# Moving four modulation blocks of the second layer from TensorE in the recurrence to VectorE sums in the gating stage

## The chip, the cores and the metric

The kernel runs on one core of one Trainium2 chip. The metric is the device time of one execution in microseconds. The engines are TensorE (PE, the matmuls), VectorE (DVE), ScalarE (ACT), GpSimd (POOL) and SyncE (SP), which here only issues DMAs. Each has its own instruction queue and works through it in order.

## The reference

Two layers over 1024 latent tokens and 256 context tokens of width 1024 (W below is 512). Each layer scales and shifts its input by a modulation of the conditioning, mixes, and closes with a gated residual and a layer norm. The change touches the modulation of the second layer (l = 1) and two branches of the first layer's mixer.

```python
def modulation(cond, w, b):
    m = jax.nn.silu(cond) @ w + b
    shift, scale, gate = jnp.split(m[:, None, :], 3, axis=-1)
    return shift, scale, gate
...
def spatial_gating(u, v, ln_g, ln_b, w_s, b_s):
    bsz, n, _ = v.shape
    vh = layer_norm(v, ln_g, ln_b).reshape(bsz, n // SGU_CHUNK, SGU_CHUNK, SGU_GROUPS, SGU_GROUP_DIM)
    s = jnp.einsum('gpq,bnqgc->bnpgc', w_s, vh) + b_s.T[:, :, None]
    return u * s.reshape(bsz, n, BRANCH_WIDTH)
...
    def branches(pp, h_rec):
        y_a = h_rec.astype(pp.dtype) * jax.nn.silu(pp[..., W:2 * W])
        u = jax.nn.gelu(pp[..., 2 * W:3 * W])
        v = jax.nn.gelu(pp[..., 3 * W:4 * W])
        y_b = spatial_gating(u, v, sgu_ln_g, sgu_ln_b, sgu_w, sgu_b) * jax.nn.silu(pp[..., 4 * W:5 * W])
        return jnp.concatenate([y_a, y_b], axis=-1) @ w_out
...
def reference(...):
    for l in range(DEPTH):
        shift, scale, gate = modulation(c, w_mod[l], b_mod[l])
        shift_c, scale_c, gate_c = modulation(c_ctx[None], w_mod[l], b_mod[l])
        h = x * (1.0 + scale) + shift
        hc = ctx * (1.0 + scale_c) + shift_c
        ...
        x = layer_norm(DEEPNORM_ALPHA * x + gate * y, ln_g[l], ln_b[l])
```

h_rec in branches is the sum of two linear recurrences (RG-LRU), one in each direction. Its coefficients come from four gates per group of 128 channels, two for each direction.

## The kernel before

**Precision and weights.** Every projection is made in three passes: an operand is split into a rounded high part and the low rest, and hi·hi, hi·lo and lo·hi are summed in PSUM. wload (L143) fetches a weight by an SP DMA into wraw (2 buffers) and splits it in two halves: the high part whi by ACT, the low part wlo by POOL (4 buffers of each, so two weights' halves). One projection (proj3c_g, L167) takes 8 k steps for each of three column chunks of 256, 512 and 512 tokens.

**PSUM.** Two three-bank slots (pj3, tag "pj") are taken in turn by whatever asks next: projections px, pg, pu, pz, the gates pgate of the recurrence, and most value tiles pv. Two single banks (psb) serve the small products.

**The recurrence stage** runs px0 and pg0 (which overlap the loading of the input), px1, rec0, pg1, px2, rec1, pg2, px3, rec2, pg3, pu0, rec3, in PE's written order (PE is under a manual schedule; the other engines are ordered by the scheduler, SP by hand in two stretches). lru_x projects and convolves one group of channels, lru_g makes its silu gate, lru_rec makes four pgate tiles of nine matmuls. For each, ACT takes a tanh out of PSUM (gt), then for each direction a tanh tt and an exponential, DVE the rest; lru_scan takes square roots on ACT and scans on DVE. pu0 is the first group's u of the gating branch, made in a three-bank slot and emptied by three gelus into ut0.

**The modulation blocks.** A layer's modulation has six blocks of 512 columns: 0 and 1 shift, 2 and 3 scale, 4 and 5 gate. The eight blocks that this stage makes are listed in `blocks`. mod_load fetches one block's eight 256 KB tiles wm. mod_do makes it on PE with eight 32-row matmuls (modp, L221) of the silu vector csil, which leave four partial sums in four groups of 32 partitions; DVE copies them to mb. At the next mod_do, mod_c closes it: for blocks 0 to 3 by four transposes (modcp, L228) and a DVE reduction, for gate blocks by one small matmul (gatep, L495). mod_step is called at steps 9 and 17 of every projection of the stage, at the start of each recurrence and after each of its directions, and every third call does mod_do.

**The gating stage** runs pz0, pu1, ten value tiles pv0 to pv9 (sgu_v), pz1, pu2, pz2, pu3, pz3. A value tile goes through a gelu on ACT (vf), mean and variance on DVE, the power -1/2 on POOL, and a scaling on DVE. sgu_s multiplies it by the 128 x 128 spatial weights (sps) between later tiles' matmuls, the last two tiles between the matmuls of pz1. Each pz ends in a tanh on ACT and two products on DVE.

**The output projection** of the first layer (out0_a, out0_b, L683 to L685) follows in six single-bank tiles pout, which are laid over the PSUM that the pj slots leave. Its eight weights w_out 0 to 7 are split by POOL for 0 to 3 and by DVE for 4 to 7 (wol, at L141).

Of the kernel before, what the change touches and what calls it, by code (L numbers as in the profile page):

```python
# [10 lines left out]
F32 = mybir.dt.float32  # L11
# [31 lines left out]
def tile_hybrid_trunk(es: ExitStack, tc: tile.TileContext, A, out, scr=None):  # L43
# [99 lines left out]
    def wload(src, nk=8, le=None):  # L143
# [3 lines left out]
        for h in range(nk // 4):  # L147
            hi = wp.tile([128, 4, 128], F32R, name="whi", tag="whi", bufs=4)
            lo = wp.tile([128, 4, 128], F32R, name="wlo", tag="wlo", bufs=4)
            split(hi, lo, raw[:, 4 * h:4 * h + 4], le=le or G)  # L150
            res.append((hi, lo))
# [73 lines left out]
    def mod_cols(mb, out, bias, one):  # L225
        p = psb("modcp")
        for i in range(4):
            T.transpose(p[:, 128 * i:128 * i + 128], mb[:, 128 * i:128 * i + 128], ident)  # L228
        t = const.tile([128, 4, 2], F32, name="mct", tag="mct", bufs=2)
        V.tensor_reduce(t, p.rearrange("p (i g r) -> p i r g", g=4, r=32)[:, :, 0:2, :], axis=AX.X, op=ALU.add)  # L230
        for o, i0, i1, b, add in zip(out, (0, 2), (2, 4), bias, one):
            V.scalar_tensor_tensor(o, t[:, i0:i1, :], add, b[:, :, None].to_broadcast([128, i1 - i0, 2]),
                                   op0=ALU.add, op1=ALU.add)
# [132 lines left out]
    with pool("lrua") as lp, pool("lruc") as lc:  # L366
# [29 lines left out]
        def lru_g(f):  # L396
            if f:
                p = pj3("pg")
                PROJ(proj3c_g(p, wload(A["w_in0"][4 + f])))
# [87 lines left out]
        def mod_c(l, blk, mb):  # L487
            if blk < 4:
                s, j = divmod(blk, 2)
                k0 = 4 * j  # L490
                mod_cols(mb, [mod1[:, k0 + 2 * i:k0 + 2 * i + 2, s, :] for i in range(2)],
                         [P("bmod1")[:, 4 * blk + 2 * i:4 * blk + 2 * i + 2] for i in range(2)], (float(s),) * 2)
            else:
# [7 lines left out]
        blocks = [(0, 4), (0, 5)] + [(1, i) for i in range(6)]  # L501
# [3 lines left out]
        def mod_step():  # L505
            calls[0] += 1
            if calls[0] % 3 == 2:
                mod_do()
# [23 lines left out]
        p = pj3("pu")  # L532
        proj3(p, wload(A["w_in0"][8]))
        for c0, n in CHUNKS:
            S.activation(ut0[:, c0:c0 + n], p[:, 256 + c0:256 + c0 + n], AF.Gelu_apprx_tanh)
# [17 lines left out]
    V.scalar_tensor_tensor(zt0, zt0, 1.0, p[:, 256:1536], op0=ALU.add, op1=ALU.mult)  # L553
    gp_cm = pool("sgu")
# [5 lines left out]
    with pool("sguw") as vw:  # L560
# [4 lines left out]
        VF = [vw.tile([128, 512], F32, name=f"vf{i}") for i in range(6)]  # L565
# [7 lines left out]
        def sgu_v(t, between=None):  # L573
# [4 lines left out]
            vf = VF[t % 6]  # L578
# [697 lines left out]
```

## Time and profile before

| | |
|---|---|
| time, median of 3 runs (lowest to highest) | 1142.79 us (1142.55 to 1142.98) |
| the profiled execution, its time | 1142.13 us |
| its span, first to last instruction | 1140.3 us |
| granted TensorE clock, mean | 0.998 |
| PE busy | 1116.7 us, 98% |
| DVE busy | 720.9 us, 63% |
| ACT busy | 436.0 us, 38% |
| POOL busy | 284.6 us, 25% |

The profiled execution lies 0.66 us below the median, and 1.8 us of its time lie outside the span. Of the span, the recurrence stage with px1 onward and up to pz0 takes from 53.2 to 204.0 us, the gating stage from 204.0 to 365.8; the output projection and the second layer follow. In a timeline row the first two numbers are the start and the duration of a row's instructions from the first start to the last end; a row with xN holds N of them. Matmuls overlap: a 512-column one shows 0.39 us and the next starts 0.23 us after it.

### The profile page before, as it was taken

Reading aid. Unit: us, or ns where it says so; the run is one execution under the profiler, and the core shown is the slowest. Engines: PE = TensorE matmul, PEld = TensorE weight load, DVE = VectorE, ACT = ScalarE, POOL = GpSimd, SP = SyncE. Lnnn points to the kernel's source line nnn. Section 1 sums busy time; section 2 is a strip of 40 time slices with the busy share of each in tenths; the row PEclk is TensorE's granted clock in tenths of the full one; section 3 lists DMA queues with packets and bytes.
Section 4 is the critical chain, followed back from the end, with each engine's and each line's share of the span. In section 5 each row is a group of like instructions: output and inputs, shape, how many; then the busy total and the mean of one; then the engine's idle time right before and its main releaser. Section 6 shows DMA issues by size and latency. Waiting matters only on the chain.

```text
span 1140.3 us, 14964 instructions
## 1 busy us (share of the span) xinstructions
PE 1116.7 (98%) x5842; PEld 920.0 (81%) x5842; DVE 720.9 (63%) x1031; ACT 436.0 (38%) x687; POOL 284.6 (25%) x228
## 2 busy tenths in 40 slices
PE   6999999999999999999999999999999999999997
PEld 4777777888888888888788788888888888888886
DVE  6777986943412566537512876777676666738986
ACT  4463665620221243343212545444544444424210
POOL 0011112530240222258402322323421321220021
PEclk9999999999999999999999999999999999999999
DMA  9654542220241543336637243442531520127641
GB/s 368 258 178 157 185 154 105 94 97 1 86 142 54 180 152 116 120 130 208 230 93 190 91 112 78 111 118 65 143 96 40 144 91 20 48 73 240 203 148 74
DMA packets 78199, 148.08 MB, mean 130 GB/s; under 512 B 6305, under 2 KB 35873, under 8 KB 77233
## 3 DMA queue, kind: packets, MB, share of 16 engines
q1 hardware_dynamic: 71088, 128.25, 33.0%
q0 software_dynamic: 7040, 18.88, 7.3%
q8 instruction: 46, 0.75, 0.3%
q14 instruction: 25, 0.20, 0.1%
HBM read 112.49 MB, written 34.62 MB: 129 GB/s over the span
## 4 chain that ended last, share of the span: by engine, by line
PE 84%; DVE 5%; DMA 4%; issue 3%; ACT 3%; POOL 1%; SPq 0%; POOLq 0%; DVEq 0%; ACTq 0%
PE pout L683 5%; PE pout L685 5%; PE pout L684 5%; PE p L184 4%; PE p L185 4%; PE p L186 4%; PE psc L992 3%; PE pv L208 3%; PE pv L209 3%; PE pv L210 3%; PE psc L993 3%; PE atr L1015 3%; PE modp L221 2%; PE pz L172 2%; PE pz L174 2%
## 5 line engine op out<-in xcount | busy, mean ns | idle before, releaser
L141 POOL TENSOR_TENSOR wlo<-wraw,whi 128x512 fp32r<-128x512 f32 x86 | 134.3, 1565 | 427.8 <-ACT whi L138 415.6
L994 DVE TENSOR_REDUCE st<-psc 128x1 f32<-128x1280 f32 x64 | 95.1, 1486 | 39.5 <-PE psc L993 39.5
L683 PE MATMUL pout<-woh,yhi 128*128 128x512 f32 (+1 forms) x296 | 114.8, 388 | 0.3 <-DVE xres L1168 0.2
L685 PE MATMUL pout<-woh,ylo 128*128 128x512 f32 (+1 forms) x296 | 114.4, 386 | 0.0
L684 PE MATMUL pout<-wol,yhi 128*128 128x512 f32 (+1 forms) x296 | 114.1, 385 | 0.0
L996 ACT ACTIVATE e<-psc,st 128x1280 f32<-128x1280 f32 x64 | 85.2, 1331 | 71.7 <-DVE st L994 68.8
L184 PE MATMUL p<-hhl,whi 128*128 128x512 f32 x256 | 105.0, 410 | 0.0
L138 ACT ACTIVATE whi<-wraw 128x512 fp32r<-128x512 f32 x92 | 57.5, 628 | 122.8 <-PE p L185 27.2
L186 PE MATMUL p<-hhl,wlo 128*128 128x512 f32 x256 | 100.5, 393 | 0.0
L185 PE MATMUL p<-hll,whi 128*128 128x512 f32 x256 | 100.3, 392 | 0.0
L138 ACT ACTIVATE ah<-atr 128x512 fp32r<-128x512 f32 (+1 forms) x96 | 47.1, 525 | 64.6 <-PE atr L1015 64.2
L992 PE MATMUL psc<-k,qh 128*128 128x512 f32 (+1 forms) x192 | 67.1, 364 | 2.6 <-ACT e L996 2.5
L993 PE MATMUL psc<-k,ql 128*128 128x512 f32 (+1 forms) x192 | 68.7, 358 | 0.0
L683 PEld LDWEIGHTS pout<-woh,yhi 128*128 128x128 f32 x296 | 55.6, 188 | 12.4 <-issue 0.6
L685 PEld LDWEIGHTS pout<-woh,ylo 128*128 128x128 f32 x296 | 55.6, 188 | 11.6 <-DVE ylo L141 0.2
L684 PEld LDWEIGHTS pout<-wol,yhi 128*128 128x128 f32 x296 | 55.7, 188 | 11.3
L138 ACT ACTIVATE yhi<-yraw 128x512 fp32r<-128x512 f32 x36 | 22.5, 631 | 108.0 <-PE pout L684 72.3
L141 DVE TENSOR_TENSOR al<-atr,ah 128x512 fp32r<-128x512 f32 (+1 forms) x96 | 54.5, 594 | 6.3 <-ACT ah L138 6.2
L186 PEld LDWEIGHTS p<-hhl,wlo 128*128 128x128 f32 x256 | 48.0, 188 | 10.8
L185 PEld LDWEIGHTS p<-hll,whi 128*128 128x128 f32 x256 | 48.3, 189 | 8.2
L184 PEld LDWEIGHTS p<-hhl,whi 128*128 128x128 f32 x256 | 48.2, 188 | 8.0
L208 PE MATMUL pv<-wvh,hhl 128*128 128x512 f32 x128 | 52.0, 406 | 0.0
(325 smaller groups left out, 2815.8 us busy)
## 6 DMA issues: line engine op xcount, KB each, us to landing
wraw<-in_w_in_dram SPq DMA_DIRECT2D x42, 512.0 KB, 3.6
wm<-in_w_mod_dram SPq DMA_DIRECT2D x64, 256.0 KB, 4.7
wraw<-in_w_out_dram SPq DMA_DIRECT2D x16, 512.0 KB, 4.3
wm<-in_w_mod_dram SPq DMA_DIRECT2D x7, 1024.0 KB, 11.4
xt<-in_xcT_dram SPq DMA_DIRECT2D x8, 640.0 KB, 8.6
xres<-in_xc_dram SPq DMA_DIRECT2D x10, 512.0 KB, 4.0
wvr<-in_w_v_dram SPq DMA_DIRECT2D x8, 512.0 KB, 3.6
n_d<-xres SPq DMA_DIRECT2D x8, 512.0 KB, 2.6
```

The source lines that it names most:

```text
L138: S.activation(hi, src, AF.Copy)
L141: le.tensor_tensor(lo, src, f32(hi), op=ALU.subtract)
L184: T.matmul(o, hi[:, k % 4], hh[:, k], start=k == 0, stop=False)
L185: T.matmul(o, hi[:, k % 4], hl_[:, k], start=False, stop=False)
L186: T.matmul(o, lo[:, k % 4], hh[:, k], start=False, stop=k == KT - 1)
L208: T.matmul(p, hh[:, k], wh, start=k == 0, stop=False)
L683: T.matmul(o, hi[:, i], wh[:, c], start=first and i == 0, stop=False)
L684: T.matmul(o, hi[:, i], wl[:, c], start=False, stop=False)
L685: T.matmul(o, lo[:, i], wh[:, c], start=False, stop=not first and i == 3)
L992: T.matmul(o, qh[:, m, cu], KS[hd, m][:, c:c + n], start=True, stop=False)
L993: T.matmul(o, ql[:, m, cu], KS[hd, m][:, c:c + n], start=False, stop=True)
L994: V.tensor_reduce(st[:, m:m + 1], p[:, 256:1536], axis=AX.X, op=ALU.max, negate=True)
```

## The change

- Blocks 0 to 3 of the second layer leave the list `blocks`, and with them their modp, modcp, DVE copies and reductions. Four gate blocks stay; mod_step makes one at every fourth call instead of every third, so they move to other calls.
- mod_sums makes the four blocks in the gating stage. For each of the eight k it loads a 256 KB tile wmd (3 buffers) and DVE adds wmd times a column of csil to macc, once for each of the two conditionings: 64 DVE operations of 128 x 512. mod_rows then sums macc over the partitions on PE with eight one-column matmuls (modq) per block and one DVE addition. In PE's order the four groups stand after pv8, pu2, pz2 and pz3.
- DVE is put under a manual schedule for the value part; two sums are written between a tile's power and its scaling, and one after it.
- The gate branch's weights (pg1 to pg3) and u0's weight get whi and wlo buffers of their own in the pool lrua, two of each.
- u0 is projected chunk by chunk into single banks (psb) instead of a three-bank slot. Five vf tiles instead of six.
- One pj tile fewer is allocated, so from rec3 on each pj tile has the other slot, and the first pout lies on the banks of pz3 instead of pu3. The pool of xres and gl (residual and gate tiles of the output projection) now reuses memory that is free only after the gating stage; in SP's order their loads stand behind the store of pz3's result and ahead of w_out 6 and 7, where before they stood among the loads of pu2 and pz2.

```diff
-    def wload(src, nk=8, le=None):
+    def wload(src, nk=8, le=None, wq=None):
...
-            hi = wp.tile([128, 4, 128], F32R, name="whi", tag="whi", bufs=4)
-            lo = wp.tile([128, 4, 128], F32R, name="wlo", tag="wlo", bufs=4)
+            hi = (wq or wp).tile([128, 4, 128], F32R, name="whi", tag="whi", bufs=2 if wq else 4)
+            lo = (wq or wp).tile([128, 4, 128], F32R, name="wlo", tag="wlo", bufs=2 if wq else 4)
...
+    def mod_sums(mw):
+        late = None
+        for blk in range(4):
+            acc = mw.tile([128, 2, 512], F32, name="macc", tag="macc", bufs=2)
+            for k in range(KT):
+                w = mw.tile([128, 512], F32, name="wmd", tag="wmd", bufs=3)
+                SY.dma_start(w, A["w_mod"][1][128 * k:128 * k + 128, 512 * blk:512 * blk + 512])
+                for c in range(2):
+                    if k == 0:
+                        V.tensor_scalar(acc[:, c], w, csil[:, k, c:c + 1], None, op0=ALU.mult)
+                    else:
+                        V.scalar_tensor_tensor(acc[:, c], w, csil[:, k, c:c + 1], acc[:, c], op0=ALU.mult, op1=ALU.add)
+                    yield
+                if k == 3 and late is not None:
+                    mod_rows(*late)
+            late = (blk, acc)
+        yield "last"
+        mod_rows(*late)
+
+    def mod_rows(blk, acc):
+        p = psb("modq")
+        s, j = divmod(blk, 2)
         for i in range(4):
...
+            for c in range(2):
+                T.matmul(p[:, 2 * i + c:2 * i + c + 1], acc[:, c, 128 * i:128 * i + 128], onesm[:, 0:1],
+                         start=True, stop=True)
+        V.scalar_tensor_tensor(mod1[:, 4 * j:4 * j + 4, s, :], p[:, 0:8].rearrange("p (i c) -> p i c", c=2),
+                               float(s), P("bmod1")[:, 4 * blk:4 * blk + 4][:, :, None].to_broadcast([128, 4, 2]),
+                               op0=ALU.add, op1=ALU.add)
...
-                PROJ(proj3c_g(p, wload(A["w_in0"][4 + f])))
+                PROJ(proj3c_g(p, wload(A["w_in0"][4 + f], wq=lp)))
...
-        blocks = [(0, 4), (0, 5)] + [(1, i) for i in range(6)]
+        blocks = [(0, 4), (0, 5), (1, 4), (1, 5)]
...
-            if calls[0] % 3 == 2:
+            if calls[0] % 4 == 2:
...
-        p = pj3("pu")
-        proj3(p, wload(A["w_in0"][8]))
+        w = wload(A["w_in0"][8], wq=lp)
         for c0, n in CHUNKS:
-            S.activation(ut0[:, c0:c0 + n], p[:, 256 + c0:256 + c0 + n], AF.Gelu_apprx_tanh)
+            p = psb("pu0")[:, 0:n]
+            proj1(p, w, c0, n)
+            S.activation(ut0[:, c0:c0 + n], p, AF.Gelu_apprx_tanh)
...
+    mw_cm = pool("modw")
+    modg = mod_sums(mw_cm.__enter__())
+
+    def mod_pass(n):
+        for _ in range(n):
+            if next(modg, "last") == "last":
+                return
...
-        VF = [vw.tile([128, 512], F32, name=f"vf{i}") for i in range(6)]
+        VF = [vw.tile([128, 512], F32, name=f"vf{i}") for i in range(5)]
...
             G.tensor_tensor(bs[:, 9:10], bs[:, 8:9], cm05[:, 0:1], op=ALU.pow)
+            mod_pass(2)
             V.tensor_scalar(vf, vf, bs[:, 6:7], bs[:, 9:10], op0=ALU.subtract, op1=ALU.mult)
             VH[t] = vf
+            mod_pass(1)
...
+        vo_cm = tc.manual_schedule(engines={nc.vector.engine})
+        vo_cm.__enter__()
         sgu_v(0)
...
         sgu_v(9, sgu_s((6, 7)))
+        vo_cm.__exit__(None, None, None)
...
         SY.dma_start(yb_d[1], zt1)
+        mod_pass(9)
...
         sgu_u(g, w)
+        mod_pass(9 if g == 2 else 20)
...
         sgu_z(g, w)
+        mod_pass(9 if g == 2 else 99)
+    run(modg)
     gp_cm.__exit__(None, None, None)
+    mw_cm.__exit__(None, None, None)
```

PE at the end of rec3, the last gate's matmuls and the start of pz0, before and then after the change:

```order
L420 MATMUL pgate<-xh,whi 128x512
L421 MATMUL pgate<-xo,whi 128x512
L422 MATMUL pgate<-xh,wlo 128x512
L495 MATMUL gatep<-mb,par 2x512
L172 MATMUL pz<-hhc,whi 128x256
L173 MATMUL pz<-hlc,whi 128x256
```

```order
L440 MATMUL pgate<-xh,whi 128x512
L441 MATMUL pgate<-xo,whi 128x512
L442 MATMUL pgate<-xh,wlo 128x512
L172 MATMUL pz<-hhc,whi 128x256
L173 MATMUL pz<-hlc,whi 128x256
L174 MATMUL pz<-hhc,wlo 128x256
```

The last closing product of a gate block (gatep) between rec3 and pz0 is gone; a second mod_do, between rec3's two directions, is gone in the same way.

DVE in the value part, the tile vf0 before, and vf2 after the change (bs is the tile of statistics; macc, wmd, csil as above):

```order
L581 BN_STATS bs<-vf_1993 128x6
L582 BN_AGGR bs<-bs 128x2
L583 TENSOR_SCALAR bs<-bs 128x1
L585 TENSOR_SCALAR vf_1993<-vf_1993,bs 128x512
L581 BN_STATS bs<-vf_1994 128x6
```

```order
L605 BN_STATS bs<-vf_1856 128x6
L606 BN_AGGR bs<-bs 128x2
L607 TENSOR_SCALAR bs<-bs 128x1
L236 SCALAR_TENSOR_TENSOR macc<-wmd,csil,macc 128x512 x2
L610 TENSOR_SCALAR vf_1856<-vf_1856,bs 128x512
L236 SCALAR_TENSOR_TENSOR macc<-wmd,csil,macc 128x512
```

Two sums stand ahead of the tile's scaling, behind its statistics, and one follows it; before, a tile's scaling came directly behind its statistics.

PE at the seam between pz3 and the output projection, with the semaphores each row waits for, before and then after:

```order
L173 MATMUL pz_2886<-hll_104,whi_2876 128x512
L174 MATMUL pz_2886<-hhl_103,wlo_2877 128x512
L683 MATMUL pout_3004<-woh0_2586,yhi_2854 128x512 [waits Activation_49]
L684 MATMUL pout_3004<-wol0_2587,yhi_2854 128x512
L685 MATMUL pout_3004<-woh0_2586,ylo_2855 128x512
```

```order
L173 MATMUL pz_2911<-hll_104,whi_2901 128x512
L174 MATMUL pz_2911<-hhl_103,wlo_2902 128x512
L249 MATMUL modq_2989<-onesm_90,macc_2742 128x1 x8
L717 MATMUL pout_3040<-woh0_2541,yhi_2879 128x512 [waits DVE_49]
L718 MATMUL pout_3040<-wol0_2542,yhi_2879 128x512
L719 MATMUL pout_3040<-woh0_2541,ylo_2880 128x512
```

Eight modq stand ahead of the first pout, and that pout waits for DVE, which reads pz3's slot last, where before it waited for ACT, the last reader of pu3's.

## Rows read from the trace of the kernel before

**Rows 1.** The page's part 1: busy us (share of the span) x instructions by engine
```profile
PE 1116.7 (98%) x5842; PEld 920.0 (81%) x5842; DVE 720.9 (63%) x1031; ACT 436.0 (38%) x687; POOL 284.6 (25%) x228
```

**Rows 2.** List of PE's waits: engine, line, releaser: us in total, times, longest
```profile
PE pgate L420 <- ACT ut L535: 1.4, 1, 1.4
```

**Rows 3.** Timeline of PE, px3 to pu0: start us, us, [idle before <-releaser]
```profile
136.33 0.28 PE L172 MATMUL px<-hhc,whi 128*128 128x256 f32 x1
...
150.08 0.60 PE L228 MATMUL modcp<-ident,mb 128*128 128x128 f32 x4
...
152.46 0.39 PE L420 MATMUL pgate<-xh,whi 128*128 128x258 f32 x1
...
158.64 0.39 PE L420 MATMUL pgate<-xh,whi 128*128 128x258 f32 x1 [0.61 <-ACT gt L424]
...
161.20 0.39 PE L172 MATMUL pg<-hhc,whi 128*128 128x256 f32 x1 [0.52 <-ACT gt L424]
...
177.56 0.28 PE L172 MATMUL pu<-hhc,whi 128*128 128x256 f32 x1
```

**Rows 4.** Timeline of PE, rec0 up to pg1
```profile
69.03 0.29 PE L420 MATMUL pgate<-xh,whi 128*128 128x258 f32 x1
...
75.10 0.39 PE L420 MATMUL pgate<-xh,whi 128*128 128x258 f32 x1 [0.33 <-ACT gt L424]
...
77.05 0.59 PE L495 MATMUL gatep<-mb,par 128*2 128x512 f32 x1
...
79.71 0.38 PE L172 MATMUL pg<-hhc,whi 128*128 128x256 f32 x1
```

**Rows 5.** Timeline of ACT in rec0: first and third gate
```profile
71.00 1.34 ACT L424 ACTIVATE gt<-pgate,hb 128x1282 f32<-128x1282 f32 x1
...
76.29 1.32 ACT L424 ACTIVATE gt<-pgate,hb 128x1282 f32<-128x1282 f32 x1
```

**Rows 6.** Timeline of PE: start of rec3, start of pz0
```profile
191.30 0.29 PE L420 MATMUL pgate<-xh,whi 128*128 128x258 f32 x1
...
203.98 0.39 PE L172 MATMUL pz<-hhc,whi 128*128 128x256 f32 x1
```

**Rows 7.** Timeline of ACT in rec3: first and third gate
```profile
194.50 1.35 ACT L424 ACTIVATE gt<-pgate,hb 128x1282 f32<-128x1282 f32 x1
...
201.38 1.33 ACT L424 ACTIVATE gt<-pgate,hb 128x1282 f32<-128x1282 f32 x1
```

**Rows 8.** Timeline of ACT beside u0's weights: a square root of rec2
```profile
178.59 1.28 ACT L442 ACTIVATE tt<-tt 128x1282 f32<-128x1282 f32 x1 [1.80 <-DVE tt L433]
```

**Rows 9.** Timeline of ACT before px1: weight split, copies out of px0
```profile
51.08 0.63 ACT L138 ACTIVATE whi<-wraw 128x512 fp32r<-128x512 f32 x1 [1.41 <-PE px L164]
...
51.94 1.08 ACT L385 ACTIVATE xp<-px 128x512 f32<-128x512 f32 x2
```

**Rows 10.** Timeline of PE: column sums of the head normalisation, then a projection
```profile
690.73 0.95 PE L1041 MATMUL pms<-onesm,sq 128*128 128x1 f32 x8
691.54 0.48 PE L184 MATMUL p<-hhl,whi 128*128 128x512 f32 x1
```

**Rows 11.** Timeline of PE: first matmul of the output projection
```profile
365.84 0.39 PE L683 MATMUL pout<-woh,yhi 128*128 128x512 f32 x1
```

**Rows 12.** Timeline of DVE from the end of pz3
```profile
367.31 1.49 DVE L646 SCALAR_TENSOR_TENSOR zt<-zt,pz 128x1280 f32<-128x1280 f32 x1 [12.25 <-ACT zt L645]
...
381.38 2.54 DVE L141 TENSOR_TENSOR wol<-wraw,woh 128x1024 fp32r<-128x1024 f32 x2 [3.70 <-ACT woh L138]
```

**Rows 13.** Timeline of DVE: scaling of the last value tile
```profile
297.75 0.55 DVE L585 TENSOR_SCALAR vf<-vf,bs 128x512 f32<-128x512 f32 x1 [0.73 <-POOL bs L584]
```

**Rows 14.** Timeline of PE: first product with the last value tile
```profile
298.83 0.60 PE L593 MATMUL sps<-wsr,vf 128*128 128x128 f32 x4
```

**Rows 15.** Timeline of POOL: low parts beside a busy and an idle DVE
```profile
212.65 14.70 POOL L141 TENSOR_TENSOR wvl<-wvr,wvh 128x512 fp32r<-128x512 f32 x6 [6.24 <-ACT wvh L138]
...
309.18 1.29 POOL L141 TENSOR_TENSOR wlo<-wraw,whi 128x512 fp32r<-128x512 f32 x1
```

More of the change, by code (lines that the diff above doesn't have):

```diff
@@ L223, in tile_hybrid_trunk @@
     sel = P("sel")
-    def mod_cols(mb, out, bias, one):
-        p = psb("modcp")
-        for i in range(4):
[L228 to L233, printed above, removed]
+    def mod_sums(mw):
[19 more added lines that the diff above has]
+        s, j = divmod(blk, 2)
+        for i in range(4):
+            for c in range(2):
[4 more added lines that the diff above has]
+                               op0=ALU.add, op1=ALU.add)
     def out_weights(op, A_w, ks, gate=None, le=None, rp=None):
@@ L487, in mod_c @@
         def mod_c(l, blk, mb):
[L488 to L493, printed above, removed]
+            if True:
                 pg = psb("gatep")
@@ L577, in sgu_v @@
                 run(between)
-            vf = VF[t % 6]
+            vf = VF[t % 5]
             S.activation(vf, p, AF.Gelu_apprx_tanh)
```

## The prediction

> **What bounds the kernel now.** I read the page first: TensorE (PE) is busy 98% of the span [rows 1], so time is saved only where PE's own instructions go, or where PE waits. PE's list of waits says how little of the second there is in this part of the kernel: the largest wait around the change is one of 1.4 us in the last recurrence, for the gelu of u0 [rows 2]. Then I read PE's timeline stage by stage, and beside it the ACT and DVE rows that release it, because work taken off PE is a gain only until the next release. The sum below is made against the profiled execution (1142.13 us with 1.8 us around its span). The median of the three runs is 0.66 higher, 1142.79; I carry the difference over to it.
>
> **What leaves the LRU stage.** One layer-1 modulation block is four transposes (modcp) and eight 32-row matmuls (modp). Outside a projection it takes PE from 150.08 to 152.46, 2.38 us. Inside one, pg3 runs from 161.20 to 177.56, 16.36 us, where a projection without a block, px3, takes 136.33 to 150.08, 13.75: 2.61 us [rows 3]. Two of the four stand inside projections and two outside: 2 x 2.38 + 2 x 2.61 = **-10.0 us** of PE. The wait for u0's gelu also goes, since u0 no longer holds one of the two three-bank slots: **-1.5**.
>
> **What becomes late in their place.** The recurrence alternates two slots, and a slot is free when ACT has read it. In rec0, which starts at 69.03, the fourth gate starts at 75.10 and its matmuls give way just before 77.05, at about 76.95, to a gate-and-modulation pair that covers PE until 79.71 [rows 4]: 1.85 us for a gate. The slot for pg1 is free when ACT ends gt3, 76.29 + 1.32 = 77.61 [rows 5]. With the pair moved into pg1, pg1 waits 77.61 - 76.95 = +0.66. In rec1 the block between the two directions goes too. What PE then meets is what rec2 shows today without one: waits of 0.61 and 0.52 for gt [rows 3]. I take 0.49 + 0.66 (rec0's own first wait is 0.33, so 0.8 to 1.2). In rec2 a gate block now stands between the directions and takes up most of those two waits, -0.9. Rec3 is the dear one. ACT has a table load there, so gt1 to the end of gt3 takes 194.50 to 202.71, 8.2 us [rows 7], against 71.00 to 77.61, 6.6 us, in rec0 [rows 5]. Today modulation blocks cover that, and pz0 starts at 203.98, 12.7 us after rec3's start at 191.30 [rows 6]. Without blocks pz0 cannot start before gt1's start (71.00 - 69.03 = 2.0 us into a recurrence) plus 8.2, that is 10.2 after rec3's start, while PE's own four gates (7.4) and one 0.49 wait take 7.9. So +0.49 and +2.3 of waiting stay. (The blocks that moved into projections are counted in neither sum; they cost PE the same there.)
>
> u0 now uses the two halves of the new weight buffers, and pg3 frees its second half only as it ends. ACT's split (0.6 us) and POOL's low part (1.3) then stand before u0's fifth k step, 1.4 us after its start: at least 0.35. ACT is in order, and the square root ahead of that split has waited 1.80 for DVE [rows 8]: at most 2.5. I take +1.2. Sum: -10.0 - 1.5 + 0.66 + 1.15 - 0.9 + 2.8 + 1.2 = -6.6 at pz0.
>
> At the very start, ACT now splits both halves of pg1's weights before it empties px0, because they have buffers of their own. Today one split precedes that and the last copy ends at 53.02, with px1 starting just behind [rows 9]. One more split, and a wait for its transfer: +0.7 (0 to 1.2). So the LRU stage gives **-5.9** (bounds -3.5 and -9).
>
> **What comes in the gating stage.** The 64 DVE sums take the place of PE work, and DVE, busy 63% of the span [rows 1], has room for their 64 x 0.6 = 38 us. What stays on PE is the closing sum over partitions: eight fp32 matmuls per block with a full 128x128 stationary operand and one column. The trace has that kind at the head normalisation: eight records from 690.73 to 691.54, 0.10 us each [rows 10]. A block has 16 records, so 1.6 to 1.7 us, and nothing hides them, for they stand between PE's back-to-back projections: 4 x 1.7 = **+6.8** (6.4, and 8.5 if a record costs what modcp's do, 0.13). The saving per block is therefore only about 0.8 us before any wait.
>
> DVE now runs in program order, and two sums stand between the variance and the scaling of each value tile. For the last tile: the scaling starts at 297.75 after 0.73 us of waiting for POOL's power [rows 13], thus the variance is out at 297.02. Two sums at 1.49 x 512/1280 = 0.60 each [rows 12] bring it to 298.22, and the scaling (0.55) ends at 298.77. PE wants it at 298.83 [rows 14]: just in time. But DVE and POOL disturb each other here: six POOL subtractions beside DVE's scan and sums took 14.70 us, 2.45 each, where one beside an idle DVE took 1.29 [rows 15]. If the power (0.55) and the sums run one after another instead of together, the scaling ends 0.5 late. I take **+0.3** (0 to 0.6).
>
> The Trainium skill speaks here against the change: its page "SBUF — State Buffer", section "Who interferes with whom", says that a DVE instruction with two SBUF inputs and a GpSimd instruction that reads SBUF exclude each other for a whole instruction. Both sums are of that kind, so by the rule this term would be 0.55 instead of 0.3 and the total 0.25 us higher; the rows on POOL agree with the direction, and no row here shows a power beside such a sum.
>
> **The seam to the output projection.** One three-bank tile fewer turns the alternation of slots over from rec3 on. Today the first pout starts with no wait, at 365.84 [rows 11], on banks of pu3 that ACT freed long before. Now it takes pz3's own banks, which DVE reads last: DVE's product starts at 367.31 and takes 1.49 [rows 12], so it ends 2.99 us after pz3. The fourth block's modq fills 1.7 of that: **+1.3** (0.8 to 1.7). The residual and gate loads, today issued long before, now stand in SP's queue ahead of the last two output weights. The low parts of those run on DVE from 381.38 to 383.92 [rows 12], just in time: a projection's 13.75 us are 60 matmuls of 512 columns, 0.229 each, and PE comes to them 78 of these after 365.84, at 383.7. Another 1 MB or so in front of them is about 3 us plus 1.3 of issuing; PE is 3 us later itself: **+0.2** (0 to 1.6).
>
> **The sum:** -5.9 + 6.8 + 0.3 + 1.3 + 0.2 = **+2.7 us**, thus 1144.8 for an execution like the profiled one and **1145.5** on the median.
>
> **Rivals.** *The waits are covered.* If ACT's order or DVE's lighter load brings the tanh rows forward, so that no gate slot is late, the 10.0 and 1.5 are gained in full but for the 1.1 us that rec2 waits today: -11.5 + 6.8 + 0.3 + 1.3 + 0.2 = -2.9, or 1139.9. For it: PE waits in few places today. Against it: ACT's spacing in rec0 and rec3 is its own work, back to back, and no mod work is on ACT. 0.2.
> *Late transfers.* The sums' 32 loads of 256 KB share SP's queue with the weights. The last load of the fourth block stands behind an output weight that waits for POOL; on DVE pz2's product stands behind the sums of that load; and pz3 takes pz2's slot when pu3 ends, one projection (13.75 us) after pz2. By the rows of today's weights that leaves some 5 us. If that chain takes over 5 us more than I think, or the last two output weights come 2 us later than I think, PE waits 2 to 4 us more: 1148.5. It decides from the point where DVE still sums the fourth block when pu3 ends. 0.1.
> *modq is cheaper.* If the weight load of one record hides under the one before, 16 records cost nearer to 1.0 than to 1.7 us, and since the wait at the seam then grows by as much for the last block, 3 x 0.7 = 2.1 us are saved: 1143.4, not measurably slower. Against it: the eight records of today are spaced by 0.10 each with the same loads. 0.15.
>
> **How the numbers follow.** The forecast as summed has 0.55, with its own bounds from 1143 to 1148. A measurement can tell about 0.2%, 2.3 us, from no change, so the ends are 1140.5 and 1145.1; the forecast lies just over the upper one. Of its 0.55 some 0.36 is above, 0.17 between, 0.02 below; of the covered waits 0.13 below and 0.07 between; the late transfers are all above; of the cheap modq 0.12 between, 0.02 below, 0.01 above. That gives faster 0.17, within 0.2% 0.36, slower 0.47. To leave out no more than 2 in 10 the range reaches from 1139.5, the covered waits, to 1149, the late transfers.
>
> **What would show it.** In the changed profile: px1 starting near 54 us; pg1 after rec0, and pz0, with a wait on ACT's gt in front; pz0 near 198 us; four groups of modq 1.7 us apart from their neighbours; the first pout with a wait on DVE zt of about 1.3 us. If pz0 starts near 193, the covered waits are right. If PE lists new waits on DMA wmd or on DVE in the value part of more than 1 us, the late transfers are. The step I trust least is the ACT-bound end of rec3 (2.3) with u0's second half (1.2): they are read from a timeline in which other work covered them.

## The result, and the profile after

The changed kernel takes 1154.6 us (median of 4 runs, 1151.9 to 1155.0) against 1142.8 before: a ratio of 1.0099, 95% interval 1.0086 to 1.0111. That is 11.8 us slower, where 2.7 were forecast, and it lies outside the range of 1139.5 to 1149. The profiled execution has a span of 1153.1 us, 12.8 more than before. TensorE's busy time on the page, which answers [rows 1], has grown by 6 us:

```profile
PE 1122.7 (97%) x5826; PEld 929.3 (81%) x5826; DVE 771.7 (67%) x1083; ACT 436.1 (38%) x687; POOL 302.5 (26%) x228
```

PE's timeline, read for where each stage starts, tells where the time went (differences of the rows in the two traces; the forecast column is the prediction's own sum):

| from ... to | before | after | difference | forecast |
|---|---|---|---|---|
| start to px1 | 53.21 | 54.36 | +1.15 | +0.7 |
| px1 to pz0 | 150.77 | 150.68 | -0.1 | -6.6 |
| pz0 to the first pout | 161.86 | 171.67 | +9.8 | +8.4 |
| first pout to the end | 774.5 | 776.4 | +1.9 | +0.2 |
| sum | | | +12.8 | +2.7 |

The list of PE's waits in the changed kernel (engine, line and releaser; us in total, times, longest) names the places. Its entries for gt stand where [rows 3] and [rows 4] had them; the one for ut of [rows 2] is gone:

```profile
PE pz L172 <- ACT gt L444: 2.0, 1, 2.0
...
PE pu L184 <- ACT whi L138: 1.8, 1, 1.8
PE pgate L440 <- ACT xp L405: 1.6, 1, 1.6
PE pgate L440 <- ACT gt L444: 1.5, 3, 0.6
PE pout L717 <- DVE zt L676: 1.2, 1, 1.2
PE pg L172 <- ACT gt L444: 1.1, 2, 0.5
...
PE pu L186 <- POOL wlo L141: 1.0, 1, 1.0
PE px L172 <- ACT xp L405: 0.3, 1, 0.3
```

The same waits in PE's timeline (start, duration, in brackets the idle time before and its releaser): px1, the second gate of rec2, two places in u0's projection, pz0, and the first pout. They answer [rows 3], [rows 6] and [rows 11]:

```profile
54.36 0.39 PE L172 MATMUL px<-hhc,whi 128*128 128x256 f32 x1 [0.34 <-ACT xp L405]
...
155.44 0.39 PE L440 MATMUL pgate<-xh,whi 128*128 128x258 f32 x1 [1.58 <-ACT xp L405]
...
179.49 0.39 PE L184 MATMUL pu<-hhc,whi 128*128 128x256 f32 x1 [1.79 <-ACT whi L138]
...
180.98 0.39 PE L186 MATMUL pu<-hhc,wlo 128*128 128x256 f32 x1 [0.99 <-POOL wlo L141]
...
205.04 0.39 PE L172 MATMUL pz<-hhc,whi 128*128 128x256 f32 x1 [1.97 <-ACT gt L444]
...
376.71 0.79 PE L717 MATMUL pout<-woh,yhi 128*128 128x512 f32 x1 [1.17 <-DVE zt L676]
```

And a row kind that the prediction did not ask for: the stretches of the trace with their granted clock (busy us of PE, PEld, DVE, ACT and POOL with their counts, then PEclk, DMA share, GB/s). Half of full speed is the 1.2 GHz level:

```profile
170.00:176.00 6.00, 6.00 (x27) 4.84 (x26) 6.00 (x4) 1.83 (x2) 4.10 (x2) 1.00 0.00 0
...
182.00:185.00 3.00, 3.00 (x11) 2.52 (x11) 2.96 (x4) 1.67 (x2) 0.00 (x0) 0.51 0.43 164
...
206.00:209.00 3.00, 3.00 (x16) 3.00 (x16) 2.96 (x3) 2.98 (x3) 1.30 (x1) 0.52 0.18 19
371.00:374.00 3.00, 3.00 (x17) 2.53 (x15) 0.00 (x0) 0.10 (x1) 0.00 (x0) 1.00 0.00 0
...
377.00:383.00 6.00, 6.00 (x15) 4.65 (x15) 3.80 (x6) 0.03 (x1) 0.00 (x0) 0.51 0.55 201
```

Three times the clock stands at about 0.5 in the changed kernel: behind the two waits in u0's projection, behind the wait at pz0, and behind the wait at the first pout, there for over 6 us. In the kernel before it is 1.00 in every one of these stages (u0's projection, pz0, the first pout):

```profile
182.00:185.00 3.00, 3.00 (x15) 2.48 (x14) 2.96 (x2) 0.94 (x1) 0.55 (x1) 1.00 0.00 0
206.00:209.00 3.00, 3.00 (x19) 2.63 (x18) 3.00 (x2) 2.97 (x3) 0.41 (x1) 1.00 0.40 109
366.00:372.00 6.00, 5.91 (x26) 4.50 (x26) 4.66 (x4) 3.13 (x3) 0.00 (x0) 1.00 0.15 61
```

What the falls cost can be read from the stages. u0's projection takes 18.91 us (176.09 to 195.00), where a projection takes 13.74 and the waits 2.78. Of the 2.4 that are left, own weight buffers make 0.3 (experiment 10), so at most 2.1 are the clock's; it may be 1.6, for in experiments 2 and 3 this projection is 0.65 and 0.81 longer than 13.74 and its wait although the clock stays at 1.00. pz0 takes 15.35 against 13.87, 1.5; the first pout to the first transpose behind the output projection takes 36.05 against 33.46, 2.6. Together that is about 6 us in the profiled execution. The other runs need not have the same: the one of 1151.9 us has a mean granted clock of 0.997, the three of 1154.4 to 1155.0 have 0.992 or 0.993.

### The profile page after: what moved, and what is told of

Same layout as the page of the kernel before. It is cut to its first block, busy times and chain, and to the rows that moved or that the text cites. A ratio compares the mean times of both kernels' runs of the same rounds, so it can differ in the third digit from the quotient of the medians.

```text
span 1153.1 us, 14990 instructions
## 1 busy us (share of the span) xinstructions
PE 1122.7 (97%) x5826; PEld 929.3 (81%) x5826; DVE 771.7 (67%) x1083; ACT 436.1 (38%) x687; POOL 302.5 (26%) x228
## 4 chain that ended last, share of the span: by engine, by line
PE 83%; DVE 7%; ACT 4%; DMA 3%; issue 2%; POOL 0%; POOLq 0%; SPq 0%; DVEq 0%; ACTq 0%
PE pout L717 5%; PE pout L718 5%; PE pout L719 5%; PE p L184 4%; PE p L185 4%; PE p L186 4%; PE pv L208 3%; PE pv L209 3%; PE pv L210 3%; PE psc L1026 3%; PE psc L1027 3%; PE atr L1049 3%; PE pz L172 2%; PE pz L174 2%; PE pz L173 2%
## 5 line engine op out<-in xcount | busy, mean ns | idle before, releaser
L141 POOL TENSOR_TENSOR wlo<-wraw,whi 128x512 fp32r<-128x512 f32 x86 | 148.0, 1727 | 432.5 <-ACT whi L138 431.4
L719 PEld LDWEIGHTS pout<-woh,ylo 128*128 128x128 f32 x296 | 56.4, 190 | 11.8 <-DVE ylo L141 0.2
```

The costliest lines, as they stand in the source:

```text
L141: le.tensor_tensor(lo, src, f32(hi), op=ALU.subtract)
L719: T.matmul(o, lo[:, i], wh[:, c], start=False, stop=not first and i == 3)
```

## The experiments

Times are medians on chips where the kernel before took 1142.1 to 1142.6 (median of a chip's runs). All edits but the two of experiment 9 are made on the changed kernel. Where two of these versions lie 2 us apart or less, their intervals overlap, and what the text says of the difference rests on the traces.

**1. The weights back in the shared buffers.**

```diff
-                PROJ(proj3c_g(p, wload(A["w_in0"][4 + f], wq=lp)))
+                PROJ(proj3c_g(p, wload(A["w_in0"][4 + f])))
...
-        w = wload(A["w_in0"][8], wq=lp)
+        w = wload(A["w_in0"][8])
```

> The changed kernel with one part undone: the gate-branch weights and u0's weight take the shared whi and wlo buffers again. Theory (own buffers let ACT's order put weight splits ahead of the copies out of px0 and px3, and tie u0's second half to the end of pg3): the waits of PE on xp (0.34 and 1.58 us) and in pu0 (1.79 and 0.99) go, and with the 2.8 us of idle PE in pu0 the stretch at granted clock 0.5 behind it, worth 1.6 us: about 6.5 us less than the changed kernel, near 1148. Rival (the recurrence simply lacks the cover of the four blocks, whatever the buffers): within 1 us of the changed kernel, 1154.

Measured: 1146.1 us, ratio 1.0033 (1.0020 to 1.0045), 8.5 less than the changed kernel. The waits on xp and in pu0 are gone. In the changed kernel ACT's rows behind px3 read:

```profile
152.99 1.15 ACT L138 ACTIVATE whi<-wraw 128x512 fp32r<-128x512 f32 x2 [8.83 <-DMA wraw<-in_w_in_dram]
154.05 0.37 ACT L403 ACTIVATE xp<-px 128x256 f32<-128x256 f32 x1
```

Two splits of pg3's weights, which have just landed, stand ahead of the copies out of px3; px3 itself had ended at 151.94. With shared buffers there is one split, and it does not wait for that transfer:

```profile
150.00 0.63 ACT L138 ACTIVATE whi<-wraw 128x512 fp32r<-128x512 f32 x1 [2.08 <-PE px L173]
150.53 0.37 ACT L403 ACTIVATE xp<-px 128x256 f32<-128x256 f32 x1
```

u0's projection then takes a plain 13.74 us, but the 2 us wait at pz0 stays (PE's rows: start of u0, start of rec3, pz0):

```profile
172.46 0.28 PE L184 MATMUL pu<-hhc,whi 128*128 128x256 f32 x1
...
186.20 0.29 PE L440 MATMUL pgate<-xh,whi 128*128 128x258 f32 x1
...
196.25 0.38 PE L172 MATMUL pz<-hhc,whi 128*128 128x256 f32 x1 [1.97 <-ACT gt L444]
```

What this wait does to the clock differs between executions. In the profiled one of this kernel, the fastest of its six runs (1144.0 us), the clock stays up behind it, where it fell behind the same 1.97 us in the changed kernel:

```profile
197.00:200.00 3.00, 3.00 (x24) 2.88 (x24) 2.96 (x3) 2.98 (x3) 1.53 (x1) 1.00 0.16 15
```

So the first theory holds, with more than it asked for. The rival falls.

**2. The two slots turned over,** so that the first pout is laid on pu3's banks again.

```diff
-            p = psb("pv") if t < 2 else pj3("pv")[:, 0:512]
+            p = psb("pv") if t < 1 else pj3("pv")[:, 0:512]
```

> The changed kernel with the alternation of the two three-bank slots turned over once (the second value tile takes a three-bank slot, not a single bank), so that the first pout lies on pu3's banks again. Theory A (the low granted clock of 0.91 in the 36 us after pz3 follows from PE's wait of 1.17 us there): wait and low clock go, 1.2 + 2.6 = 3.8 us less than the changed kernel, 1150.8. Theory B (it follows from the one-column matmuls of modq, which keep PE as little busy): only the wait goes, 1.2 us less, 1153.4, and the clock falls there still.

Measured: 1151.6 us, ratio 1.0077 (1.0062 to 1.0092), 3.0 less; the interval overlaps that of the changed kernel a little. The wait at the first pout is gone, and with it the fall of the clock, though the sixteen records of modq stand there as before:

```profile
374.00:377.00 3.00, 3.00 (x14) 2.45 (x14) 2.97 (x7) 1.39 (x2) 0.00 (x0) 1.00 0.00 0
377.00:383.00 6.00, 6.00 (x29) 4.95 (x28) 2.20 (x2) 0.00 (x0) 0.00 (x0) 1.00 0.83 282
```

Theory A holds: modq alone does not bring the clock down in this trace; with the wait of 1.17 behind it, the clock fell in all four traces that have both (the changed kernel, experiments 1, 3 and 7). A part of the gain goes to a new wait for the last output weights, which PE now reaches earlier:

```profile
PE pout L718 <- DVE wol L141: 0.9, 2, 0.5
```

**3. The gate blocks put where PE waits for ACT.** mod_step's calls 4, 11, 18 and 23 stand between the two directions of the four recurrences, 24 behind the last.

```diff
-            if calls[0] % 4 == 2:
+            if calls[0] in (4, 11, 18, 23, 24):
```

> The changed kernel with the four gate blocks at other calls: between the two directions of rec0, rec1, rec2 and rec3 and after rec3, where PE waits on ACT. Theory (the waits on gt of 0.32, 0.54, 0.61, 0.55, 0.61 and 1.97 us are there because no block covers them, and the low clock after the last one follows from it): about 4.6 + 1.5 = 6 us less than the changed kernel, 1148.5, the xp and pu0 waits left. Rival (the blocks cost PE the same there and new waits on DMA wm or on gt take their place): within 1.5 us of 1154.

Measured: 1141.9 us, ratio 0.9993 (0.9984 to 1.0002), 12.7 less than the changed kernel, twice the expectation. Every wait on gt is gone; rec3 ends like this, a block between its directions and one small product ahead of pz0, no wait:

```profile
187.36 0.63 PE L221 MATMUL modp<-wm,csil 128*32 128x512 f32 x3
...
193.73 1.02 PE L510 MATMUL gatep<-mb,par 128*2 128x512 f32 x2
194.68 0.39 PE L172 MATMUL pz<-hhc,whi 128*128 128x256 f32 x1
```

pz0 starts at 194.68, 10.4 us earlier than in the changed kernel. The waits on gt make 4.6 of that. The wait on xp (1.58) is gone too, but not because the block in rec2 covers it: the block stands behind the gate that waited. The transfer of pg3's weights has another place. In the changed kernel SP issues it behind two stores of ya (first row), 3.1 us before px3 ends, and it lands 1 us after that end; here (second row) it goes ahead of them and lands before px3 ends, so that the two splits, which stand ahead of the copies here as well, hold nothing up:

```profile
148.85 0.37 SPq L145 DMA_DIRECT2D wraw<-in_w_in_dram  x1
...
139.11 0.33 SPq L145 DMA_DIRECT2D wraw<-in_w_in_dram  x1
```

The first wait in pu0 is gone (1.79) and with it the fall of the clock there; the second has grown from 0.99 to 1.50. So some of the waits of experiment 1 were removed by another means: the gains of the two do not add.

**4. All three edits.**

> The three edits of the runs before at once. If the parts add: 6.5 + 6 + 1.2 to 3.8 us less than the changed kernel, 1138 to 1141, faster than the kernel before by 2 to 4 us. If the waits only change places, or the clock falls elsewhere: 1145 or more.

Measured: 1136.7 us, ratio 0.9947 (0.9932 to 0.9961): 18.0 less than the changed kernel and 5.9 less than the kernel before beside it (1142.5). The single gains sum to 24.2; the 6 us between are about what experiments 1 and 3 both remove (1.58 on xp, 1.79 in pu0 and the fall of the clock behind it).

**5. The last recurrence alone left bare,** in the version of experiment 4.

```diff
-            if calls[0] in (4, 11, 18, 23, 24):
+            if calls[0] in (4, 11, 18, 19, 22):
```

> The three-edit version (1136.7) with the last recurrence alone left bare again: the block between its directions goes to the end of rec2, the last small product to its start. Theory: PE waits 0.6 us at its fourth gate and 2 us at pz0 as in the changed kernel, and the granted clock falls to 0.5 for about 3 us behind the longer wait: 2.6 + 1.5 = 4.1 us more, 1140.8. Rival (the fall of the clock in the changed kernel came from several waits together, in pu0 and in rec3): 2.6 us more at most, 1139.3, and the clock stays up.

Measured: 1143.4 us, ratio 1.0010 (1.0001 to 1.0020), 6.7 more than with the cover, more than either theory said. PE's rows show the wait at pz0 again, and ahead of it one that I had made myself: the block moved to the end of rec2 came before its weights had landed, so that it took 6.2 us instead of 2.7:

```profile
155.11 1.31 PE L221 MATMUL modp<-wm,csil 128*32 128x512 f32 x3 [0.79 <-DMA wm<-in_w_mod_dram]
...
197.44 0.39 PE L172 MATMUL pz<-hhc,whi 128*128 128x256 f32 x1 [1.97 <-ACT gt L444]
```

The clock falls behind pz0 once more, with no trouble in u0 ahead of it:

```profile
197.00:200.00 3.00, 2.56 (x14) 2.56 (x15) 2.93 (x3) 3.00 (x4) 1.72 (x1) 0.67 0.00 0
200.00:203.00 3.00, 3.00 (x17) 2.82 (x17) 2.46 (x2) 2.97 (x3) 0.00 (x0) 0.76 0.65 214
```

pz0 takes 15.40 us, 1.5 more than in the version with cover. So rec3's own waits (0.61 and 1.97) are enough for the fall in this execution; the rival, several waits together, is not needed. The excess divides into 2.6 of waits, 1.5 of clock and 3.6 of the misplaced block. That is 7.7, where the two profiled executions (1144.6 and 1137.1) lie 7.5 apart and the medians 6.7.

**6. DVE's value part left to the scheduler,** in the version of experiment 4.

```diff
-        vo_cm = tc.manual_schedule(engines={nc.vector.engine})
-        vo_cm.__enter__()
...
-        vo_cm.__exit__(None, None, None)
```

> The three-edit version with DVE's value part ordered by the scheduler, not in program order. It puts a dozen sums ahead of the first value tile's statistics. Theory: DVE, in order, stands at sums whose 256 KB tiles have not landed (3 us each), the value tiles' scaling comes late and PE waits at the first group of sps: 1 to 6 us more than 1136.7. Rival (the value tiles have so much slack that the order does not matter): within 0.5 us of it.

Measured: 1155.9 us, ratio 1.0115 (1.0100 to 1.0131), 19.2 more. The theory's place was right and its size was not (1 to 6 us). The list of PE's waits has one new entry:

```profile
PE sps L619 <- DVE vf L610: 15.0, 4, 4.9
```

DVE stands at the first sum, whose tile has not landed, and reaches the first value tile's statistics at 237.45 instead of 224.07:

```profile
228.40 0.88 DVE L234 TENSOR_SCALAR macc<-wmd,csil 128x512 f32<-128x512 f32 x2 [8.45 <-DMA wmd<-in_w_mod_dram]
```

The granted clock is 0.50 from 245 to 261 us and near that again from 306 to 309, behind these waits of 2.3 to 4.9 us; it is where the other 4 us most likely went.

The written order, which I had listed as a risk, is what keeps the sums out of the value tiles' way.

**7. The slots not turned over,** in the version of experiment 4 (the edit of experiment 2 taken out).

> The three-edit version without the turned slots: the first pout lies on pz3's banks. Theory: PE waits 1.2 us behind the last modq and the granted clock falls to 0.5 there, 1 to 2.6 us more, less the 1.1 us that PE waits for the last output weights in the three-edit version: 1 to 2.7 us more, 1137.7 to 1139.4. Rival (modq alone brings the clock down, or the late output weights weigh as much as the wait): the same as 1136.7 within 0.5 us.

Measured: 1137.8 us, ratio 0.9962 (0.9948 to 0.9976), 1.1 more, as the theory said, but inside the intervals. The clock falls at the seam again, behind modq and the wait of 1.17 us, but for a shorter time than in the changed kernel:

```profile
356.00:359.00 3.00, 2.96 (x22) 2.68 (x20) 0.41 (x1) 1.68 (x2) 0.00 (x0) 1.00 0.00 0
359.00:362.00 3.00, 1.87 (x5) 1.48 (x6) 2.96 (x7) 1.45 (x2) 0.00 (x0) 0.72 0.00 0
362.00:365.00 3.00, 3.00 (x11) 2.39 (x10) 2.26 (x2) 0.00 (x0) 0.00 (x0) 0.71 0.82 254
```

**8. SP's order at the seam written by hand,** on top of experiment 4: the manual order of the queue runs from the last four output weights to the first out0_b, which puts the last two weights ahead of the residual tiles.

```diff
+    so2_cm = tc.manual_schedule(engines={nc.sync.engine})
+    so2_cm.__enter__()
     wob_cm = pool("wo0b")
...
     out0_b(0)
+    so2_cm.__exit__(None, None, None)
```

> The three-edit version with SP's order at the seam written by hand, so that the last two output weights are asked for ahead of the residual tiles and the context gates. Theory: the three-edit version's two waits on wol (0.37 and 0.77 us) come from the weights' place in SP's queue behind those loads; they go, 1.1 us less than 1136.7, 1135.6. Rival (DMA traffic, not the place in the queue, sets the landing, or the residual tiles now come late instead): within 0.5 us of 1136.7, with a wait on DVE or DMA in another place.

Measured: 1135.6 us, ratio 0.9940 (0.9926 to 0.9953). The waits for wol are gone; the gain of 1.1 over experiment 4 is the theory's and lies inside the intervals. This version has the lowest time and is called the best version below: 7 us faster than the kernel before, 19 faster than the changed one.

**9. What of that is the move to DVE?** Two runs on the kernel before, with all eight blocks left on PE in the recurrence. The first takes only u0's projection into single banks (and turns the slots back).

> The kernel before, all eight modulation blocks left in the recurrence, with u0 alone projected chunk by chunk into single banks, and the alternation of the three-bank slots kept as it was by giving the second value tile a three-bank slot. Theory: PE's wait of 1.45 us for u0's gelu goes and nothing else changes: 1141.3. If that were all that the three-edit version gains over the kernel before (6 us), it would come to 1137, and moving the blocks to DVE would be worth nothing.

Measured: 1140.5 us, ratio 0.9984 (0.9975 to 0.9994); the theory's number was 1141.3. The second also puts its blocks where PE waits:

```diff
-            if calls[0] % 3 == 2:
+            if calls[0] in (4, 7, 11, 13, 16, 18, 21, 23, 24):
```

> The version with u0 alone in single banks (1140.5; all eight blocks in the recurrence, none on DVE), its blocks put to the calls where PE waits for ACT, a block between the directions of every recurrence among them. Theory: its waits of 0.33, 0.62 and 0.54 us go, 1.5 us less, 1139.0; the best version so far (1135.6) then owes some 3.4 us to the sums on DVE: 10 us of blocks less 6.8 us of one-column matmuls. Rival (with enough cover the place of the four blocks is worth nothing): 1136 to 1137.

Measured: 1139.3 us, ratio 0.9971 (0.9961 to 0.9981), no wait on gt left. Between the best of either kind lie 3.6 us, near the 3.2 that 10.0 of blocks less 6.8 of modq make. The stages of the two traces show both terms apart: px1 to pz0 takes 147.09 us with eight blocks (53.12 to 200.21) and 136.90 with four (53.57 to 190.47), 10.2 less; pz0 to the first pout takes 161.86 (to 362.07) and 168.88 (to 359.35), 7.0 more. So the exchange of PE work that the change rests on is real and small.

**10. Which of the own buffers costs?** The best version with those of the gate branch alone, then with those of u0 alone.

> The best version (1135.6) with the gate branch's weights alone in buffers of their own, as in the changed kernel; u0's stay shared. Theory: ACT's order again puts two splits ahead of the copies out of px0 and px1 starts some 0.5 to 1.2 us later, the blocks cover the wait at px3: 0.5 to 1.5 us more, 1136.1 to 1137.1. Rival (all of the cost of own buffers lies in u0): 1135.6.

Measured: 1137.3 us, ratio 0.9955 (0.9940 to 0.9970), 1.6 more than the best, with intervals that overlap. There is no wait at px3: the two splits stand ahead of the copies again, but the transfer has landed in time, as in experiment 3.

> The best version with u0's weights alone in buffers of their own. With two buffers used by u0 only, its splits need not wait for pg3. Theory (the wait in pu0 is there because pg3 and u0 share one pair of halves): no wait in pu0, within 0.5 us of 1135.6. Rival (ACT's place for u0's splits, behind the square roots, makes the wait): 1.5 to 3 us more.

Measured: 1135.8 us, ratio 0.9944 (0.9929 to 0.9959), not to be told from the best. No wait in pu0 appears, where experiment 3, with pg3 and u0 on one pair of halves, has one of 1.50: it comes of the sharing. The gate branch's own buffers cost the later px1 (a wait on xp of 0.4 us), and each of pg1 to pg3 takes 14.04 us there instead of 13.69 to 13.77 without any wait listed. u0's projection with own buffers takes 14.06 instead of 13.74, so it pays the same third of a microsecond. It is spread evenly: a 512-column matmul shows 396 ns on average instead of 389, and the next one starts 0.233 us after it instead of 0.227. What makes that was not found.

## Why the prediction was wrong

The direction was right and the size was not: 2.7 us forecast, 11.8 measured. By the prediction's own steps:

**The blocks removed, -10.0: right.** Experiment 9 shows 10.2, and 7.0 more in the stage that modq lies in. **modq, +6.8: right to the tenth.** A group takes 1.70 us from its first record to the next projection's matmul, at the first three places alike (the fourth has the seam's wait behind it):

```profile
290.49 1.84 PE L249 MATMUL modq<-onesm,macc 128*128 128x1 f32 x16
292.19 0.47 PE L208 MATMUL pv<-wvh,hhl 128*128 128x512 f32 x1
```

**The value tile, +0.3: nothing.** The last tile's scaling starts at 302.53 behind the two sums and ends at 303.07,

```profile
301.21 1.40 DVE L236 SCALAR_TENSOR_TENSOR macc<-wmd,csil,macc 128x512 f32<-128x512 f32 x2
302.53 0.54 DVE L610 TENSOR_SCALAR vf<-vf,bs 128x512 f32<-128x512 f32 x1
```

and PE's product with it starts at 303.12 with no idle time before it:

```profile
303.12 0.60 PE L619 MATMUL sps<-wsr,vf 128*128 128x128 f32 x4
```

It is as close as the sum said, 0.05 us. POOL's power beside the sums took 0.92 us instead of 0.55, and the two sums still took 1.40 together. The power starts just behind the first sum and ends 0.44 us after that sum does (301.21 and 0.70 make 301.91; 301.43 and 0.92 make 302.35). It is 0.44 to 0.47 in all nine tiles that have a sum there. So it looks as if the power waits for the running sum and gets in before the second; since the scaling stands behind the second sum anyway, this costs nothing. With more work on POOL the wait is seen on DVE too: the two sums beside this subtraction took 3.55 us, and the second ended 0.56 us after it.

```profile
317.97 2.77 POOL L141 TENSOR_TENSOR wol<-wraw,woh 128x1024 fp32r<-128x1024 f32 x1 [0.69 <-ACT woh L138]
...
317.75 3.55 DVE L236 SCALAR_TENSOR_TENSOR macc<-wmd,csil,macc 128x512 f32<-128x512 f32 x2
```

The trace agrees with the rule that the prediction quoted from the Trainium skill ("SBUF — State Buffer", section "Who interferes with whom"). What the prediction made of it, 0.55 us, was too much, since the power gets in between the two sums and neither of them takes longer for it. A POOL subtraction of 128 x 512, which takes 1.29 us beside an idle DVE [rows 15], took 9.75 beside a DVE that runs its instructions back to back (first row; the second is the power):

```profile
162.70 9.75 POOL L141 TENSOR_TENSOR wlo<-wraw,whi 128x512 fp32r<-128x512 f32 x1 [6.49 <-ACT whi L138]
...
301.43 0.92 POOL L608 TENSOR_TENSOR bs<-bs,cm 128x1 f32<-128x1 f32 x1 [7.84 <-DVE bs L607]
```

**The wait at the seam, +1.3: right,** 1.17. **The last output weights, +0.2:** no wait in the changed kernel, 0.9 and 1.1 us once the seam's wait was removed (experiments 2 and 4).

**The LRU stage, -6.6 at pz0: the step that failed;** it came to -0.1. Of its terms, the waits on gt were right: 0.54 after rec0 for 0.66, 0.61 and 0.55 in rec1 for 1.15, 0.61 and 1.97 in rec3 for 2.8. Three others were not.
- *u0's weights.* I took 1.2 between 0.35 and 2.5; the waits were 1.79 and 0.99, 2.78. The mechanism was the one named, and this was one of the two terms that the prediction trusted least. Its size was wrong because I took the middle, where the rows pointed at the upper end: the square root ahead of the split ended 2.3 us after u0's start before [rows 3, rows 8]. Here it ended 2.8 after it (176.09), having waited 3.70 for DVE, with the split and POOL's low part behind it:

```profile
177.64 1.27 ACT L462 ACTIVATE tt<-tt 128x1282 f32<-128x1282 f32 x1 [3.70 <-DVE tt L453]
178.82 0.61 ACT L138 ACTIVATE whi<-wraw 128x512 fp32r<-128x512 f32 x1
...
179.51 1.42 POOL L141 TENSOR_TENSOR wlo<-wraw,whi 128x512 fp32r<-128x512 f32 x1 [3.84 <-ACT whi L138]
```

- *px3's copies.* I had seen at px0 that own buffers let the scheduler put a second split ahead of the copies, and had not asked the same at the three other projections px. At px3 the two splits stand ahead of the copies too, and they wait for the transfer of their weights, which SP issues late (experiment 3), so that rec2's second gate waits 1.58 us. I had forecast -0.9 for rec2, from a gate block between its directions. Only the closing product of a block stands there (0.94 us); rec2's own waits are gone with it, and yet the stage is +1.3 (10.02 us from rec2 to pg3 against 8.74).
- *The gate branch's projections* are 0.3 us longer each with own buffers, and so is u0's, 1.3 us in all; the change to them was costed at nothing but the split order.

The later px1 (+1.15 for +0.7) is no miss: px1 starts between 53.07 and 54.18 in the ten traces without own buffers for the gate branch, and between 53.95 and 54.43 in the four with them.

**The clock, about 6 us: missing altogether.** Of 10.1 us between the forecast and the profiled span, this is more than half. I summed every wait of PE at its own length. In this kernel, where PE is busy for hundreds of microseconds at 1.00, a wait of 1.8 to 2 us (or the pair of 1.79 and 0.99 in u0's projection) was in most traces followed by 3 to 4 us at the lower level, and the seam's wait of 1.17 behind modq by 3 to 6. The lower level halves PE's work (15 matmuls from 377 to 383 us in the changed kernel, 29 in experiment 2) and so cost 1.5 to 2.6 us again. Nothing in the kernel before could have shown it there, since its longest wait in these stages is 1.45 us and its clock is 1.00 behind it. But it does not follow every time: the wait of 1.97 at pz0 brought the clock down in the changed kernel and in experiments 2 and 5, and not in the profiled run of experiment 1; a single wait of 1.58 (changed kernel), 1.52 (experiment 2) or 1.50 (experiment 3) did not, one of 1.80 in experiment 2's rec2 did, with 0.71 over the next 6 us. The Trainium skill ("TensorE: Matmul & The Clock Gate", section "What's actually happening") says that the slow level is the default, that activity releases it, and that the same kernel shows different numbers of slow matmuls from run to run; the traces agree in kind, with 0.52 and 1.00 behind the same wait. How much inactivity it takes was not settled here.

**The rivals.** "The waits are covered" was the opposite of what happened, but it is what experiment 3 builds: the cover that I had counted as lost can be had back by choosing the calls. That its 1139.9 is near the 1141.9 measured there is chance: experiment 3 still pays a wait of 1.50 in pu0 and the seam, and without them (experiment 4) the time is 1136.7. "Late transfers" did not occur: PE lists no wait on wmd and none on DVE in the value part; DVE itself waited 3.4 and 1.2 us for wmd, and PE did not feel it. Experiment 6 shows how dear such waits are where the order is another. "modq is cheaper" fell.

The parts that came out dearer sum to 11.8 (6.2 of clock at most, 2.2 at rec2, 1.6 at u0, 1.3 in the projections with own buffers, 0.45 at the start), those that came out cheaper to 1.0 (0.3 on the gt waits, 0.3 at the value tile, 0.1 at the seam, 0.2 for the last output weights). The difference, 10.8, is 0.7 more than the miss of 10.1. The clock's part in u0 may be 0.5 smaller, as said above, and the kernel before has a wait of 0.6 in its second layer (on qf) that the changed one has not.

## What to carry to other kernels

Before work is taken off a busy engine, list what it covers: here four blocks of 2.5 us were worth 3 us net of their replacement, and the place of the four that stayed was worth 12.7 in the changed kernel, part of it waits that the shared buffers remove as well. Price a wait on a busy TensorE as more than its length, since the clock may fall behind it as it did here, and look for the granted clock of the stretches behind every new wait. A buffer of its own for a transfer or a split can make things worse without any contention: what may start earlier was put earlier into ACT's queue, ahead of the copy that frees a slot, and held it up where its transfer was late.

## What the runs showed of the hardware that was not expected

- A wait of 1.8 to 2 us of a TensorE that had been busy at clock 1.00 was followed by a fall of the clock within the next microseconds at five of the six places looked at (0.50 to 0.76 over stretches of 3 us: u0 and pz0 in the changed kernel, rec2 and pz0 in experiment 2, pz0 in experiment 5); one of 1.97 us was not (1.00, experiment 1).
- Sixteen one-column matmuls without a wait behind them left the clock at 1.00 (experiment 2); with a wait of 1.17 us behind them it fell to between 0.50 and 0.72 over stretches of 3 us, in four traces of four.
- A POOL subtraction of 128 x 512 took 1.29 us beside an idle DVE and 9.75 beside DVE operations back to back; a 128 x 1 power took 0.55 alone and 0.92 to 1.04 beside a sum, ending 0.44 to 0.47 us after that sum. Two sums of 128 x 512 took 1.40 us, and 3.55 beside a POOL subtraction of 128 x 1024.
- Eight fp32 matmuls with a full stationary operand and one column take 1.70 us up to the next projection's matmul, the same at three places.
